# Landing the rotary tables as half runs on 64 partitions and packing them with shuffles and copies

## The chip, the cores and the metric

One core of a Trainium2 chip runs one launch of the kernel. The time is the device time of that launch in microseconds. The profile comes from one execution and gives the span of its work, about 2 us less than the time.

## The reference

A rotary embedding on the first half of each head, with tables of 512 x 32 floats of which only the first 16 columns are used:

```python
# x: (16, 512, 16, 64) float32; cos, sin: (512, 32) float32
x1, x2 = x[..., :32], x[..., 32:]
first  = x1[..., :16] * cos[..., :16] - x1[..., 16:] * sin[..., :16]
second = x1[..., :16] * sin[..., :16] + x1[..., 16:] * cos[..., :16]
return concatenate([first, second, x2], axis=-1)
```

## The kernel before

The 8192 rows of 4 KB are cut into four tiles of 8 MB, 128 partitions by 16 rows (K = 16). A ring of three tiles lies in SBUF. SyncE issues all loads and stores in one queue; VectorE rotates in place; GpSimd issues the two table loads. Partition p of a tile needs the table rows of partition p modulo 32, so the table is landed on 32 partitions and copied to the four groups.

```python
K = 16; T = 4; PB = S // K   # 32
REP = P // PB                # 4
cosf = cos.rearrange("(p k) j -> p (k j)", k=K)       # 32 rows of 2 KB
stage = const_pool.tile([PB, 2, K, HF], fp32)
table = const_pool.tile([P, 2, K, 2, Q], fp32)
# ... (cut)
nc.gpsimd.dma_start(out=stage[:, 0]..., in_=cosf)
nc.gpsimd.dma_start(out=stage[:, 1]..., in_=sinf)
load(0, 0, K0); load(0, K0, K); load(1); load(2, 0, KC)
for r in range(REP):
    nc.vector.tensor_copy(out=table[r * PB : (r + 1) * PB]..., in_=stage[...])
# rotate(): b = x1*s; x1 = x1*c; x1a -= b2; x1b += b1   (four VectorE instructions)
rotate(0, 0, K0); rotate(0, K0, (K0 + K) // 2); rotate(0, (K0 + K) // 2, K)
store(0)
load(2, KC, K)
load(3)                       # takes the place of tile 0, waits for store(0)
for t in range(1, T):
    rotate(t, 0, KC); rotate(t, KC, K); store(t)
```

## Time and profile before

| | before |
|---|---|
| time, median of the first 3 runs | 162.19 us (161.71 to 162.36) |
| span of the profile | 160.1 us |
| DMA queue of the x loads and stores | 97.8% of 16 engines' span |
| VectorE busy | 110.0 us, 69% |
| tables landed, first rotation, first store issued | 9.13, 11.94, 44.14 us |

The lines are shown in the prediction. In them DVE is VectorE, POOL is GpSimd and SPq is SyncE's queue of instructions; q1 is the queue of the x loads and stores and q0 that of the table loads, each with its packets, MB and share of the 16 engines' span.

### The profile page before, as it was taken

What the parts mean: (1) busy time and instruction counts of PE and PEld (TensorE: products, weight loads), DVE (VectorE), ACT (ScalarE), POOL (GpSimd) and SP (SyncE); (2) the same over time, 40 slices, a digit from 0 to 9 for tenths busy, and PEclk for the clock granted to TensorE, in tenths of its full rate; (3) what the DMA queues carried; (4) which work ended last, traced back from release to release, by engine and by line L of the source; (5) the groups of instructions that cost most, each with busy time, mean ns of one, the idle gap of its engine ahead of it and who ended that gap; (6) DMA issues with size and microseconds to landing.
All of it is one profiled execution on the core that took longest, in us unless ns stands there. A gap on an engine that the chain in (4) does not pass through costs nothing.

```text
span 160.1 us, 109 instructions
## 1 busy us (share of the span) xinstructions
DVE 110.0 (69%) x40; POOL 1.3 (1%) x6
## 2 busy tenths in 40 slices
DVE  0069709999999999999999994799999900000000
POOL 3000000000000000000000000000000000000000
DMA  6999999699699799899996996996996996996991
GB/s 197 385 504 454 393 459 524 262 524 491 295 401 581 328 524 409 377 393 418 483 540 295 491 524 262 524 524 262 524 524 262 524 524 262 524 491 295 524 459 66
DMA packets 1504, 67.24 MB, mean 420 GB/s; under 512 B 192, under 2 KB 192, under 8 KB 224
## 3 DMA queue, kind: packets, MB, share of 16 engines
q1 hardware_dynamic: 1440, 67.11, 97.8%
q0 software_dynamic: 64, 0.13, 0.2%
HBM read 33.69 MB, written 33.55 MB: 420 GB/s over the span
## 4 chain that ended last, share of the span: by engine, by line
DMA 50%; DVE 28%; DVEq 1%; issue 0%; SPq 0%
DMA ring<-in_x_dram 32%; DMA out_dram<-ring 18%; DVE b_t L83 10%; DVE ring L84 10%; DVE ring L85 5%; DVE ring L88 3%; DVEq L127 1%; SPq L53 0%; DVEq L83 0%
## 5 line engine op out<-in xcount | busy, mean ns | idle before, releaser
L83 DVE TENSOR_TENSOR b_t<-ring,table 128x4096 f32<-128x4096 f32 (+2 forms) x9 | 35.6, 3959 | 8.2 <-DMA ring<-in_x_dram 8.0
L84 DVE TENSOR_TENSOR ring<-ring,table 128x4096 f32<-128x4096 f32 (+2 forms) x9 | 35.6, 3950 | 0.3
L85 DVE TENSOR_TENSOR ring<-ring,b_t 128x2048 f32<-128x2048 f32 (+2 forms) x9 | 18.4, 2049 | 0.3
L88 DVE TENSOR_TENSOR ring<-ring,b_t 128x2048 f32<-128x2048 f32 (+2 forms) x9 | 18.4, 2042 | 0.0
L67 DVE COPY table<-stage 32x1024 f32<-32x1024 f32 x4 | 2.7, 684 | 9.2 <-DMA stage<-in_sin_dram 9.1
L58 POOL DMA_DIRECT2D stage<-in_cos_dram x1 | 0.6, 631 | 0.8 <-PEq L127 0.8
L59 POOL DMA_DIRECT2D stage<-in_sin_dram x1 | 0.5, 498 | 0.0
L116 POOL MEMSET const-bfloat16-1.0<- 128x1 bf16 x1 | 0.1, 102 | 0.0
L116 POOL MEMSET const-float32-0.0<- 128x1 f32 x1 | 0.1, 99 | 0.2 <-issue 0.2
L116 POOL MEMSET const-float32-1.0<- 128x1 f32 x1 | 0.1, 99 | 0.0
L116 POOL MEMSET const-uint8-127<- 128x1 uint8 x1 | 0.1, 99 | 0.0
## 6 DMA issues: line engine op xcount, KB each, us to landing
ring<-in_x_dram SPq DMA_DIRECT2D x2, 4096.0 KB, 43.9
ring<-in_x_dram SPq DMA_DIRECT2D x1, 6144.0 KB, 22.4
ring<-in_x_dram SPq DMA_DIRECT2D x1, 2048.0 KB, 8.5
stage<-in_cos_dram POOLq DMA_DIRECT2D x1, 64.0 KB, 6.0
stage<-in_sin_dram POOLq DMA_DIRECT2D x1, 64.0 KB, 7.2
out_dram<-ring SPq DMA_DIRECT2D x4, 36.4
ring<-in_x_dram SPq DMA_DIRECT2D x2, 35.0
```

The costliest lines, as they stand in the source:

```text
L58: nc.gpsimd.dma_start(out=stage[:, 0].rearrange("p k j -> p (k j)"), in_=cosf)
L59: nc.gpsimd.dma_start(out=stage[:, 1].rearrange("p k j -> p (k j)"), in_=sinf)
L67: nc.vector.tensor_copy(out=table[r * PB : (r + 1) * PB].rearrange("p t k c j -> p (t k) c j"), in_=stage.rearrange("p t k j -> p (t k) j" ...
L83: nc.vector.tensor_mul(out=b_t, in0=x1, in1=s)
L84: nc.vector.tensor_mul(out=x1, in0=x1, in1=c)
L85: nc.vector.tensor_sub(out=x1[:, :, :, 0:Q], in0=x1[:, :, :, 0:Q], in1=b_t[:, :, :, Q:HF])
L88: nc.vector.tensor_add(out=x1[:, :, :, Q:HF], in0=x1[:, :, :, Q:HF], in1=b_t[:, :, :, 0:Q])
L116: nc = _bacc.Bacc("TRN2", target_bir_lowering=False, num_devices=1)
L127: with _tile.TileContext(nc) as tc:
```

## The change

Its intent is to land each table in 64 rows of 1 KB on 64 partitions in place of 32 rows of 2 KB on 32. Row u of the 64 is half h = u mod 2 of the run of partition u / 2, so the halves have to be brought side by side again. Two shuffles gather the even rows and the odd rows within each group of 32 partitions; two copies bring the upper group's result to partitions 0 to 31 and then overwrite 0 to 15 with the lower group's.

```diff
-    cosf = cos.rearrange("(p k) j -> p (k j)", k=K)
-    sinf = sin.rearrange("(p k) j -> p (k j)", k=K)
+    cosf = cos.rearrange("(u k) j -> u (k j)", k=K // 2)
+    sinf = sin.rearrange("(u k) j -> u (k j)", k=K // 2)
...
-    stage = const_pool.tile([PB, 2, K, HF], fp32)
+    stage = const_pool.tile([2 * PB, 2, K // 2, HF], fp32)
+    spun = const_pool.tile([2 * PB, 2, 2, K // 2, Q], fp32)
+    packed = const_pool.tile([PB, 2, 2, K // 2, Q], fp32)
...
+    for h in range(2):
+        nc.vector.stream_shuffle(
+            out=spun[:, h].rearrange("p t k j -> p (t k) j"),
+            in_=stage.rearrange("p t k j -> p (t k) j")[:, :, 0:Q],
+            mask=[2 * (j % (PB // 2)) + h for j in range(PB)],
+        )
+    for q in (1, 0):
+        n = PB // 2 * (q + 1)
+        nc.vector.tensor_copy(
+            out=packed[0:n], in_=spun[q * PB : q * PB + n].rearrange("p h t k j -> p t h k j")
+        )
...
-            in_=stage.rearrange("p t k j -> p (t k) j")[:, :, 0:Q]
+            in_=packed.rearrange("p t h k j -> p (t h k) j")
```

## The prediction

> **What bounds the kernel now.** I began with the page: its busy shares, its queue lines and its chain.
>
> ```profile
> span 160.1 us, 109 instructions
> DVE 110.0 (69%) x40; POOL 1.3 (1%) x6
> ...
> q1 hardware_dynamic: 1440, 67.11, 97.8%
> q0 software_dynamic: 64, 0.13, 0.2%
> HBM read 33.69 MB, written 33.55 MB: 420 GB/s over the span
> ...
> DMA 50%; DVE 28%; DVEq 1%; issue 0%; SPq 0%
> ```
>
> VectorE is busy for 69% of the span, but the queue that SyncE feeds (all x loads and all stores) has the 16 DMA engines busy for 97.8% of it. So the data transfers are the bound. The chain shows DVE at 28%, which looks as if VectorE time counted. It is misleading here: the chain follows semaphores (a load, the rotation, the store that waits for it), and a store's wait for the rotation costs nothing if the DMA engines still have older work queued. Whether they do is answered by the busy time in stretches (columns: stretch, its length, DVE, POOL, clock, DMA share, GB/s).
>
> ```profile
> 9.20:24.00 14.80, 9.95 (x9) 0.00 (x0) 1.00 1.02 443
> 24.00:44.00 20.00, 19.83 (x8) 0.00 (x0) 1.00 0.97 419
> 44.00:72.00 28.00, 27.76 (x10) 0.00 (x0) 1.00 1.00 431
> 72.00:101.00 29.00, 25.72 (x8) 0.00 (x0) 1.00 1.05 452
> ```
>
> The DMA share is 1.0 within the rounding of stretches from the ninth microsecond on, whatever VectorE does. The packet records of the trace say the same more sharply: from the first packet, 2.0 us into the span, to the last, 156.9 us later, no instant has the queue empty, and the engines hold 16 packets in flight nearly throughout. A 64 KB packet takes 2.42 us; 67.1 MB are 64 such packets on each of 16 engines, which is 155 us of the 160. The end is set by bytes.
>
> The third view is the timeline of the start, which is where the change acts.
>
> ```profile
> 1.25 0.63 POOL L58 DMA_DIRECT2D stage<-in_cos_dram  x1 [0.81 <-PEq L127]
> 1.88 0.50 POOL L59 DMA_DIRECT2D stage<-in_sin_dram  x1
> 9.13 2.77 DVE L67 COPY table<-stage 32x1024 f32<-32x1024 f32 x4 [9.13 <-DMA stage<-in_sin_dram]
> ...
> 17.74 1.21 DVE L88 TENSOR_TENSOR ring<-ring,b_t 128x1024 f32<-128x1024 f32 x1
> 23.66 3.37 DVE L83 TENSOR_TENSOR b_t<-ring,table 128x3072 f32<-128x3072 f32 x1 [4.71 <-DMA ring<-in_x_dram]
> ...
> 42.37 1.75 DVE L88 TENSOR_TENSOR ring<-ring,b_t 128x1536 f32<-128x1536 f32 x1
> 44.14 0.35 SPq L56 DMA_DIRECT2D out_dram<-ring  x1
> ```
>
> Two margins follow. **First margin, 4.71 us:** VectorE gets the tables at 9.13, copies them, rotates the first quarter of tile 0 until 18.95, then sits idle until the rest of tile 0 lands at 23.6. Work added before 18.95 eats this idle time first. **Second margin, some 6.5 us:** the first store is issued at 44.14, but the loads issued before it are not through then. Loads of 20 MB (two tiles of 8 MB and half a third) stand before it, and their last packets end about 50.3 us after the first, at 52.4 us; the store's first packets start at 52.0. From issue to first packet the first load took 1.3 us (0.74 to 2.0), so the store could be issued until about 50.7 without an empty queue: 50.7 less 44.14 is 6.5 us. Later stores have more: the last is issued at 128.1, and its first packet starts at about 139.
>
> **What the Trainium skill says.** Four places bear on the change.
>
> "VectorE: DVE Perf Modes", section "The perf-mode tier table": an fp32 tensor copy in SBUF runs two elements a cycle, a stream shuffle one, about 2400 ns for 2048 elements. The trace agrees for the copy: 1024 elements took 684 ns, while a tensor-tensor on 1024 took 1212, so half the slope on the same fixed part. The shuffle is not in this trace.
>
> "Vector Engine (DVE) Microarchitecture Reference", section 3.8: the shuffle's 32 mask bytes are loaded by an instruction of their own, all banks of 32 lanes apply the same mask, and an operation on at most 32 partitions may read one quadrant and write another. This explains the form of the change: the shuffle cannot bring lanes of quadrant 1 to quadrant 0, so two copies follow. The trace agrees as to moves across quadrants: the four table copies of one quadrant into each of four all take 680 to 686 ns.
>
> "DMA: Bandwidth & Descriptors", section "Queues, rings and completion order": each DMA engine goes round its queues packet by packet. The trace agrees: a table's 4 KB packet took 159 ns, yet the tables landed 6.0 and 7.2 us after issue, since each of their packets waited behind a 16 KB or 48 KB packet of x.
>
> "SBUF — State Buffer", section "SBUF: two separate sides": a VectorE operation in a two-port mode locks GpSimd out of writing descriptors. It cannot matter here: GpSimd has ended its two issues at 2.4 us, and the first VectorE instruction, before and after the change, waits for what these bring.
>
> **The change part by part.** *Moved, the table loads.* Each is still 64 KB on 16 engines, 4 KB an engine, now as 64 rows of 1 KB in place of 32 rows of 2 KB. In DMA time both tables are 32 packets of 0.16 us over 16 engines, 0.3 us an engine; I expect that unchanged, and if the shorter rows doubled it, 0.3 us more. The issue on GpSimd may grow from 0.63 and 0.50 us by some tenths for twice the rows. Landing: unchanged if 4 KB remain one packet; I take 0.3 us later.
>
> *Added, two shuffles.* Each handles 2 tables by 8 rows by 16 columns = 256 elements a partition. At one element a cycle: the tensor-tensor rows give (2292 - 1212)/1024 = 1.05 ns an element and some 140 ns fixed, so 256 x 1.05 + 140 = 0.41 us. From the page's 2400 ns at 2048 the fixed part would be 250 ns and the shuffle 0.52 us. I take 0.46, two of them 0.92. Two mask loads have no duration in the trace; I put 0.1 us for each, 0.2 together, as a guess.
>
> *Added, two copies to 32 and 16 partitions.* 512 elements each; partitions work in parallel, so the smaller one costs the same. From 684 ns for 1024 at two elements a cycle (half of 1.05 ns, so 538 + 146): 512 x 0.525 + 146 = 0.41 us, two 0.83. Were the reordered source to fall to one element a cycle, 0.68 each, which is half a microsecond more in all.
>
> *Kept, the four replications.* Still 32x1024, from a contiguous source now: 684 ns each.
>
> *Removed.* Nothing from VectorE, no byte from the DMA.
>
> Sum on VectorE: 0.92 + 0.20 + 0.83 = 1.95 us, and 0.3 us of later landing: 2.25 us. All of it lies between the landing of sin and the first rotation, which would start at 14.2 in place of 11.94 and end at 21.2 in place of 18.95. The idle time before the second rotation falls from 4.71 to about 2.5 us and that rotation still starts at 23.66 by its load. From there on nothing moves: the first store at 44.1, the end by the DMA bytes. Sum on the path that sets the end: 0, or up to 0.3 if short rows cost DMA time.
>
> **The rivals.** *A, the tables land much later.* If the 64 rows made two packets an engine, each table would wait for one more packet of x; a 48 KB packet takes 1.82 us, so up to 3.6 us for both. With 1.95 us of VectorE work that is 5.6 us, 0.9 beyond the first margin: the first store would be issued at 45.0, still before 50.7. Time: 162.2. For it speaks the slow landing before; against it, that the bytes per engine stay the same.
>
> *B, VectorE becomes the bound at the start.* To reach the end of the kernel the addition must exceed 4.71 + 6.5 = 11.2 us, five times my sum; each microsecond beyond would then cost one. Slower by 2% needs 3.2 us more, 14.4 in all. Nothing in the profile hints at that.
>
> *C, the change pays.* Tables on 64 partitions might land sooner, as the change seems to hope. Even landing at zero would only lengthen the 4.71 us of idle time, since the second rotation starts with its x load. Time: 162.2.
>
> *D, a change of DMA rate.* Different SBUF addresses or another die could move the 2.42 us a packet; the table rows themselves are 0.13 of 67.2 MB. Nothing speaks for it; a tenth of a percent is 0.16 us.
>
> **Range and chances.** The centre is the median before, 162.19, plus nothing: 162.2. The three runs spread from 161.71 to 162.36, that is -0.5 to +0.2; I widen this for another occasion and for up to 0.3 us of DMA time: 161.5 to 163.0. Two per cent would be 3.2 us. Faster would need fewer bytes, and there are none: 0.01. Slower needs rival B: 0.015. Within 2%: 0.975.
>
> **What would show it right or wrong.** Right: the four replications start near 11.4 and keep 684 ns; shuffles of 0.4 to 0.55 us and copies near 0.41; the idle time before the second rotation near 2.5 us, its start still at 23.6 to 23.7; the first store at 44.1; q1 at about 97.8% and 420 GB/s; DVE busy near 112 us. Wrong as to a step: copies near 0.68 (no double rate), sin landing more than a microsecond later (rival A), replications unequal to 684. Wrong altogether: a first store after 50.7, a stretch with a DMA share well below 1 after the ninth microsecond, or a packet time other than 2.42 us.

## The result and the profile after

The changed kernel took 162.31 us (median of 6 runs, 161.75 to 162.52), the kernel before 161.89 us in the same rounds (6 runs). The ratio is 1.0016, with a 95% interval of 0.9995 to 1.0037: no difference is resolved. Ratios here are the mean time of one kernel's fast runs over that of the other's of the same rounds, so they are not quite the ratio of the quoted medians.

The page of the changed kernel, the lines that answer to those of before:

```profile
span 160.1 us, 115 instructions
DVE 111.6 (70%) x46; POOL 1.4 (1%) x6
...
q1 hardware_dynamic: 1440, 67.11, 97.6%
q0 software_dynamic: 64, 0.13, 0.2%
...
DMA 50%; DVE 28%; DVEq 1%; issue 0%; SPq 0%
```

Six instructions and 1.6 us of VectorE work have come in. The span, the packets and bytes of both queues and the shares of the chain are as before. Where the new work went is seen in the timeline of the start (start, duration, engine, line, operation, names, shapes, and in brackets the idle time before it).

```profile
1.89 0.52 POOL L61 DMA_DIRECT2D stage<-in_sin_dram  x1
8.98 0.01 DVE L71 LOAD_MASK_SELECT spun<-stage  x1 [8.98 <-DMA stage<-in_sin_dram]
9.01 0.43 DVE L71 STREAM_SHUFFLE spun<-stage 64x256 f32<-64x256 f32 x1
9.36 0.01 DVE L71 LOAD_MASK_SELECT spun<-stage  x1
9.36 0.43 DVE L71 STREAM_SHUFFLE spun<-stage 64x256 f32<-64x256 f32 x1
9.82 0.86 DVE L78 COPY packed<-spun 32x512 f32<-32x512 f32 x2
10.72 2.77 DVE L83 COPY table<-packed 32x1024 f32<-32x1024 f32 x4
13.53 2.30 DVE L99 TENSOR_TENSOR b_t<-ring,table 128x2048 f32<-128x2048 f32 x1
...
23.37 3.37 DVE L99 TENSOR_TENSOR b_t<-ring,table 128x3072 f32<-128x3072 f32 x1 [2.83 <-DMA ring<-in_x_dram]
...
43.85 0.35 SPq L58 DMA_DIRECT2D out_dram<-ring  x1
```

From the landing of sin to the first rotation it now takes 13.53 - 8.98 = 4.55 us; before it was 11.94 - 9.13 = 2.81. The addition is 1.74 us. The first rotation ends 1.59 us later (20.54 against 18.95), and the idle time after it has shrunk from 4.71 to 2.83 us. The second rotation does not start later: its load sets its start, and that landed 0.29 us earlier in this execution. That is scatter and no gain: in runs below that begin with the same table stage, this rotation starts between 23.31 and 23.73. The first store is issued at 43.85 us, no later than before.

### The profile page after: what moved, and what is told of

Its sections match the earlier page's. It is cut to its first block, busy times and chain, and to the rows that moved or that the text cites. A ratio compares the mean times of both kernels' runs of the same rounds, so it can differ in the third digit from the quotient of the medians.

```text
span 160.1 us, 115 instructions
## 1 busy us (share of the span) xinstructions
DVE 111.6 (70%) x46; POOL 1.4 (1%) x6
## 4 chain that ended last, share of the span: by engine, by line
DMA 50%; DVE 28%; DVEq 1%; issue 0%; SPq 0%
DMA ring<-in_x_dram 32%; DMA out_dram<-ring 18%; DVE b_t L99 10%; DVE ring L100 10%; DVE ring L101 5%; DVE ring L104 3%; DVEq L143 1%; SPq L55 0%; DVEq L99 0%
## 5 line engine op out<-in xcount | busy, mean ns | idle before, releaser
L83 DVE COPY table<-packed 32x1024 f32<-32x1024 f32 x4 | 2.7, 683 | 0.1
L78 DVE COPY packed<-spun 32x512 f32<-32x512 f32 (+1 forms) x2 | 0.8, 416 | 0.1
L71 DVE STREAM_SHUFFLE spun<-stage 64x256 f32<-64x256 f32 x2 | 0.8, 430 | 0.0
```

Source lines behind the costliest of these rows:

```text
L71: nc.vector.stream_shuffle(out=spun[:, h].rearrange("p t k j -> p (t k) j"), in_=stage.rearrange("p t k j -> p (t k) j")[:, :, 0:Q], mask= ...
L78: nc.vector.tensor_copy(out=packed[0:n], in_=spun[q * PB : q * PB + n].rearrange("p h t k j -> p t h k j"))
L83: nc.vector.tensor_copy(out=table[r * PB : (r + 1) * PB].rearrange("p t k c j -> p (t k) c j"), in_=packed.rearrange("p t h k j -> p (t h ...
```

## The experiments

My theory was: the bytes through the DMA queue set the end, and what VectorE does before the first store is hidden by two margins in turn, the idle time before the second rotation and the work still queued when the first store is issued. The main rival was that VectorE's chain sets the end (the chain of the profile gives it 28%) and that only the idle time hid the addition. Chips differed between the batches, so each run is compared with the kernel before in its own rounds; those medians were 162.01, 162.06 and 161.84 us.

### Nothing on VectorE at the start: no_table_stage

```diff
-    for r in range(REP):
-        nc.vector.tensor_copy(out=table[...], in_=stage[...])
+    nc.vector.memset(table, 1.0)
```

> The kernel before with the four replications and their wait for the tables taken away; a memset at the start fills the table instead (wrong result on purpose; the table loads stay, unread). My theory: the first rotation starts when the first quarter of tile 0 lands, near 9.2 us, in place of 11.94; the idle time before the second rotation grows from 4.71 to about 7.4 us; time 162.2, ratio 1.00. Rival (the table stage counts, so undoing it pays): 2.8 us less, 159.4, ratio 0.983.

Measured: 162.01 us, ratio 1.0003 (0.9986 to 1.0020). Its timeline:

```profile
9.36 2.30 DVE L77 TENSOR_TENSOR b_t<-ring,table 128x2048 f32<-128x2048 f32 x1 [7.42 <-DMA ring<-in_x_dram]
...
23.68 3.37 DVE L77 TENSOR_TENSOR b_t<-ring,table 128x3072 f32<-128x3072 f32 x1 [7.32 <-DMA ring<-in_x_dram]
```

The whole table stage can vanish and the time stays; the 2.6 us gained turn into idle time before the second rotation. So no other way of landing or packing the tables can pay in this kernel, however good. (The table loads themselves stayed; their packets are 0.3 us of each DMA engine's time.)

### Less of VectorE's work everywhere: less_vector

```diff
-        nc.vector.tensor_sub(out=x1[:, :, :, 0:Q], ...)
-        nc.vector.tensor_add(out=x1[:, :, :, Q:HF], ...)
```

> The changed kernel without the subtraction and the addition of each rotation (wrong result on purpose): VectorE loses 18 instructions and 36.8 of 111.6 us. My theory: the first store is issued some 7 us earlier, the queue was full anyway, the DMA share stays near 0.98, time 162.2, ratio 1.00. Rival (the 28% of VectorE in the chain that ended last are on the path): up to 10 us less, 152, ratio 0.94.

Measured: 162.19 us, ratio 1.0008 (0.9991 to 1.0025). The page:

```profile
DVE 75.2 (47%) x28; POOL 1.4 (1%) x6
...
q1 hardware_dynamic: 1440, 67.11, 97.7%
...
DMA 54%; DVE 19%; SPq 0%; issue 0%
```

VectorE lost 36 us and its share of the chain fell from 28 to 19%, while the time stayed. So the chain's VectorE share was not time that sets the end. The chain follows who released whom, and does not show that the released store then stood in a queue.

### Fewer bytes: less_bytes

```diff
-        store(t)
+        store(t, 0, K if t < T - 1 else KC)
```

> The changed kernel whose last store leaves out the second half of its rows, 4 MB of 64 (wrong result on purpose: the rest of the output is not written). My theory: the end moves by what 8 packets of 32 KB on each engine take, 8 x 1.21 = 9.7 us: 152.5, ratio 0.940. Rival (the last store waits for VectorE, whose last rotation ends at 128 us, so the tail is latency): clearly less than 9.7 us.

Measured: 152.83 us, ratio 0.9431 (0.9417 to 0.9445). That is 9.2 us less (0.0569 of 162.06) where 9.7 was worked out from the packets. Leaving out bytes moves the end nearly one for one, and nothing else tried shortened it.

### More work before the first rotation: after_rep2, after_rep3, after_rep4, after_rep6, before_rep6

Each repeats the four replications, which keeps the result correct and adds 2.8 us of VectorE work a time. after_rep2 was run after the other four, whose results its expectation quotes. The edit of after_rep3, the others alike:

```diff
-    for r in range(REP):
+    for r in [i % REP for i in range(4 * REP)]:
```

> The changed kernel with the replications three times over (8 more copies, 5.5 us more VectorE work). The first store should be issued near 46.6 us, 4 us before the point where the queue runs dry. By the two margins alone: 162.2, ratio 1.00. The run with 8.3 us more had no hole in the queue and was yet 1.5 us longer, with the last 64 KB packets before the two switches of direction near 70 and 98 us stretched from 2.42 to up to 3.75 us; if that sets in as soon as the first margin is gone, this run is about 0.5 to 1.0 us longer than the kernel before, ratio 1.003 to 1.006.

> The changed kernel with its four replications done four times over in place of once: 12 more copies at 0.69 us, 8.3 us more VectorE work ahead of the first rotation, same result. My theory (DMA bytes set the end, VectorE has two margins): 2.83 us of idle time before the second rotation are left, so that rotation starts 5.5 us late, the first store is issued near 49.3 us in place of 43.85, still before about 50.7, the queue never runs dry, time 162.2 (ratio to the kernel before 1.00). Rival (VectorE's chain sets the end, and the change was hidden only by the idle time before the second rotation): 5.5 us longer, about 167.7, ratio 1.034.

> The changed kernel with the replications five times over: 16 more copies, 11.1 us more VectorE work. My theory: first store issued near 52.1 us, about 1.4 us past the point (some 50.7) from which the queue runs dry; this is near the knee, so time 162.2 plus 0.3 to 1.8, ratio 1.002 to 1.011. Rival (VectorE's chain sets the end): 8.2 us longer, 170.4, ratio 1.05.

> The changed kernel with the replications seven times over: 24 more copies, 16.6 us more VectorE work. My theory: first store issued near 57.6 us, 6.9 us past the point where the queue runs dry, so the time is 162.2 + 6.9 = 169.1, ratio 1.043, and the trace shows a hole of nearly 7 us in the DMA work from about 52 us. Rival (VectorE's chain sets the end): 13.8 us longer, 176, ratio 1.085. Third theory (DMA bound whatever VectorE does): 162.2.

> The kernel before with the replications seven times over, 16.6 us more VectorE work: past both margins, so that what the change adds can be seen. My theory: first store near 56.0 us, 5.3 us past the point where the queue runs dry, time 167.5; and the changed kernel with the same addition is longer by what the change adds ahead of the first rotation, 1.6 us (169.1). If the change's cost were hidden by something other than the two margins, the two would take the same time.

Measured, with the hole (the time in which no packet of the x queue is under way) and the number of 64 KB packets of over 2.8 us (of 768) from the packet records:

| kernel | first store issued, us | hole, us | long packets | longest, us | time, us | ratio |
|---|---|---|---|---|---|---|
| changed kernel | 43.85 | none | 0 | 2.69 | 162.31 | 1.0016 |
| after_rep2 | 47.08 | none | 1 | 2.90 | 162.43 | 1.0034 |
| after_rep3 | 49.75 | none | 20 | 3.75 | 163.53 | 1.0093 |
| after_rep4 | 52.31 | 1.43 | 32 | 3.77 | 165.36 | 1.0205 |
| after_rep6 | 58.02 | 7.09 | 32 | 4.13 | 172.32 | 1.0631 |
| before_rep6 | 56.58 | 5.43 | 33 | 4.31 | 170.42 | 1.0514 |

The hole can be seen in the busy time by stretches. First after_rep6 (columns as in the prediction: DVE, POOL, clock, DMA share, GB/s), then before_rep6:

```profile
44.00:52.00 8.00, 7.90 (x5) 0.00 (x0) 1.00 0.91 393
52.00:59.00 7.00, 6.93 (x4) 0.00 (x0) 1.00 0.33 140
59.00:72.00 13.00, 12.90 (x5) 0.00 (x0) 1.00 0.94 408
```

```profile
44.00:52.00 8.00, 7.93 (x4) 0.00 (x0) 1.00 0.91 393
52.00:57.00 5.00, 4.93 (x4) 0.00 (x0) 1.00 0.00 0
57.00:72.00 15.00, 14.90 (x5) 0.00 (x0) 1.00 1.01 437
```

In before_rep6 nothing moves from 52 to 57 us, since the loads are through and the first store has not come. In after_rep6 the table's exact hole is the better figure; the 0.33 of its stretch are packets that start at the very end of it, from 58.86 us, and are counted with their whole time where they start.

Three things follow. **First, the theory of two margins comes nearer than both rivals.** VectorE's chain as the bound would have made after_rep3, rep4 and rep6 5.5, 8.2 and 13.8 us longer; they were 1.5, 3.3 and 10.2 longer by the ratios. A kernel bound by DMA whatever VectorE does would have stayed at 162. The holes were forecast well (1.4, 6.9 and 5.3 us expected for after_rep4, after_rep6 and before_rep6), but the times of the four with a first store after 49 us all came out above what I had expected: 163.53 against 162.2, 165.36 against 162.5 to 164.0, 172.32 against 169.1, 170.42 against 167.5. **Second, the cost of the change can be seen once the margins are used up.** With the same repetitions in both, the changed kernel was 1.8 us longer than the kernel before (mean 172.28 against 170.45; the two profiled executions alone differ by 1.3 us in span), and its added instructions take 1.74 us. **Third, my figure for the second margin was too generous.** The store's first packet follows its issue by 0.84 us when the queue is empty (after_rep4, after_rep6 and before_rep6 alike), and the first engine is free at 51.70 us in the kernel before, so the queue runs dry only when the store comes after 50.9 us. But after_rep3, with its store at 49.75 and no hole, already lost 1.5 us, and the runs with a hole lost about 2 to 3 us beyond it (10.2 against 7.1, 8.3 against 5.4, 3.3 against 1.4). A good part lies in stretched packets: the last 64 KB packet of each engine before the switch from storing to loading near 70 us, and before the one from loading to storing near 98 us. Their excess over 2.42 us, summed and divided by 16 engines, is 0.2 and 0.9 us in after_rep3. That is a mean, and the end is that of the slowest engine: the last packets of the 16 engines end 1.7 us apart there, 0.6 apart in the changed kernel.

### What stretches the packets: rep3_light, busy_tail, late_store2

Besides the late first store itself (theory 3), two other things differ near 98 us in after_rep3: VectorE is busy there (theory 1), and the store of tile 2 is not yet queued (theory 2). late_store2 was meant to hold that store back.

```diff
 rep3_light = after_rep3 and, in rotate():
+        if t > 0:
+            return
         nc.vector.tensor_sub(...)
```

```diff
 busy_tail
         store(t)
+        if t == 2:
+            nc.vector.tensor_mul(out=b_full, in0=ring[:, 2, 0:KC, :, 0:HF], in1=Sn...)
```

```diff
 late_store2
         rotate(t, 0, KC)
+        if t == 3:
+            nc.vector.tensor_scalar_mul(out=cell, in0=cell, scalar1=1.0)   # one column of tile 2
+            store(2)
         rotate(t, KC, K)
-        store(t)
+        if t != 2:
+            store(t)
```

> The changed kernel with the replications four times over, and without the subtraction and addition from tile 1 on (wrong result on purpose): the first store is as late as in the run with four replications (49.7 us), but VectorE is done with tile 2 near 85 us, so its store is queued and VectorE is idle when the last load ends near 100 us. If the stretched packets near 98 us come of VectorE being busy then (theory 1) or of the next store not being queued yet (theory 2), they are gone: 0.9 of the 1.5 us go, ratio about 1.003. If they come of the late first store itself (theory 3), they stay: ratio about 1.009.

> The changed kernel with one more 128x4096 multiplication into the scratch buffer after the store of tile 2 is issued (97.6 us), so that VectorE is busy over the end of the last load, and the store is queued in time (correct result). Theory 1 (busy VectorE stretches the last packets): up to 0.9 us longer, ratio 1.005. Theories 2 and 3: 162.2, ratio 1.00.

> The changed kernel whose store of tile 2 is held back until the first half of tile 3 is rotated (near 115 us in place of 97.6), by a multiplication of one column of tile 2 by one (correct result); the queue still holds the store of tile 1 until 120 us. Theory 2 (the next store must be queued when the direction switches): 0.9 us longer, ratio 1.005, with stretched packets near 98 us. Theories 1 and 3: 162.2, ratio 1.00.

Measured: rep3_light 164.51 us, ratio 1.0161 (1.0125 to 1.0197); busy_tail 162.11, ratio 1.0016 (1.0001 to 1.0031); late_store2 162.12, ratio 1.0019 (1.0004 to 1.0034).

The edit of late_store2 did not do what it was meant to. Two stretches of its timeline:

```profile
57.55 0.15 DVE L118 TENSOR_SCALAR ring<-ring 128x1 f32<-128x1 f32 x1
...
98.00 0.34 SPq L58 DMA_DIRECT2D out_dram<-ring  x1
```

The multiplication ran at 57.55 us, before tile 2 was rotated, and the store of tile 2 was issued at 98.00 and not near 115, hardly later than the changed kernel's 97.64. (Why it ran so early is not shown; its column is one that no rotation writes.) So this run does not test theory 2. after_rep2 does:

```profile
98.55 2.28 DVE L104 TENSOR_TENSOR ring<-ring,b_t 128x2048 f32<-128x2048 f32 x1
100.86 0.34 SPq L58 DMA_DIRECT2D out_dram<-ring  x1
```

There VectorE was busy over the switch near 98 us and the store of tile 2 came only at 100.86, and yet one packet alone in the whole run took over 2.8 us (2.90, at 108 us).

The timeline of rep3_light shows that its store of tile 2 was queued early and VectorE idle over the switch:

```profile
91.34 0.34 SPq L58 DMA_DIRECT2D out_dram<-ring  x1
103.28 4.43 DVE L99 TENSOR_TENSOR b_t<-ring,table 128x4096 f32<-128x4096 f32 x1 [11.96 <-DMA ring<-in_x_dram]
```

Yet its stretched packets near 98 us were there, with 1.1 us of excess, and the time was longer still than after_rep3's. In busy_tail no packet took over 2.7 us, and its ratio is the changed kernel's own 1.0016. So theories 1 and 2 fall: rep3_light has the stretched packets without either of their causes, and after_rep2 has both causes with hardly a stretched packet. The loss goes with a first store that is issued late against the loads queued before it, setting in between 47.1 us (after_rep2, whose ratio of 1.0034, 1.0019 to 1.0049, cannot be told from the changed kernel's) and 49.75 us. SyncE issues the load of the rest of tile 2 0.39 us behind that store in each of these kernels, so no run tells the late store from this late load. Why the engines stretch a packet some 20 and 50 us after that stays open; no run here shows its mechanism.

### The shuffle's rate: wide_shuffle

```diff
+    nc.vector.stream_shuffle(
+        out=table[0:64]...,                       # 1024 elements, overwritten later
+        in_=ring[0:64, 0, 0]..., mask=list(range(32)))
```

> The changed kernel with one more shuffle, of 1024 elements on 64 partitions, from the first rows of tile 0 into the table ahead of its replication (correct result). It measures the slope of a shuffle: if it goes at the rate of a tensor-tensor (1.05 ns an element, 140 to 160 ns fixed) it takes 1.22 to 1.24 us beside 0.43 for 256 elements; if the fixed part is larger[...], 1.3 or more. Time unchanged, 162.2, as 1.3 us fit in the 2.83 us of idle time.

One look (a single run, state unknown): 162.19 us, correct. The timeline:

```profile
9.32 0.43 DVE L76 STREAM_SHUFFLE spun<-stage 64x256 f32<-64x256 f32 x1
...
12.10 1.28 DVE L70 STREAM_SHUFFLE table<-ring 64x1024 f32<-64x1024 f32 x1
```

The wide shuffle took 1.28 us: (1.28 - 0.43)/768 = 1.11 ns an element and 0.15 us fixed, an estimate from two shuffles of one execution that read differently laid out tiles. That lies between what I had put down for the two theories: the fixed part is the small one, and the slope is a little above a tensor-tensor's 1.05 ns.

## Why the prediction was right

The time was forecast at 162.2 us and measured at 162.31; by the ratio the change does nothing that 6 runs resolve. (A cost of some 0.3 us stays possible: busy_tail and late_store2, with the changed kernel's table stage, have intervals that just exclude 1.) The agreement of the time does not test the sum of the added work, since a sum of double the size would have been hidden as well; the timeline tests it. The steps:

- **The bound.** Right, and shown twice: less_bytes moved the end by nearly what the missing packets take, and less_vector did not move it at all.
- **The sum of the added work.** Forecast 1.95 us, measured 1.74. The copies were right (0.416 and 0.415 us against 0.41); with 683 ns for 1024 elements that is 0.52 ns an element, so the half slope, which one size could only suggest, is now shown. The shuffles took 0.43 us each against 0.46, and the second starts 0.35 us after the first, so that they overlap a little. The mask loads, a guess of 0.1 us each, are 5 to 14 ns. The replications stayed at 683 ns and began at 10.72 us in place of 11.4.
- **The landing.** Forecast 0.3 us later; sin landed 7.0 us after its issue in place of 7.2. As the forecast said, the packets stayed the same in number and size (64, 0.13 MB), and rival A's extra packet did not come about. The issue on GpSimd grew by only 0.02 us each. The reason that the prediction gives for the slow landing covers only a part of it: in the packet records of the kernel before, the first table packet starts at 5.34 us, 4.1 us after the issue of cos, and from there on table packets stand behind 16 KB packets of x of 0.6 to 0.9 us, none behind one of 48 KB. What fills the 4.1 us is not shown.
- **The first margin.** Forecast to shrink to about 2.5 us, measured 2.83; the difference is the smaller sum and the landing, less 0.3 us by which the x load came early.
- **The second margin.** It was not needed for the result: the first store came at 43.85 us. The prediction's packet times lie some 0.25 us late on the profile's axis (the first x packet starts at 1.75 us and not at 2.0, the first store packet at 51.7 and not at 52.0); this cancels in the 50.7 us. Tested by itself it was too large as I had put it. "Each microsecond beyond would then cost one" left out the stretched packets: after_rep3 lost 1.5 us before the queue ran dry, and before_rep6, with 17.2 us more than the kernel before ahead of the first rotation, lost 8.3 us where the two margins' 11.2 us would have left 6.0.
- **Rival C.** no_table_stage, which has no table stage at all, shows that no better landing could have paid.

## What to carry to other kernels

Before costing an added instruction, find out what stands in the queue behind which its result will wait: if the DMA engines hold work until well after the store is issued, VectorE work is free up to that point, and neither a 69% busy engine nor its share of the chain of releases says otherwise. Take the margin as smaller than the moment at which the queue would run dry, as coming close to it already cost about 1% here. And when the queue is full from its first packet to its last, look to the bytes first: moving fewer of them was the only edit here that made the kernel faster. A higher rate of the packets was not tried.

## What the Trainium skill lacked or had wrong

- "Vector Engine (DVE) Microarchitecture Reference", section 3.8, names the instruction that loads the shuffle's mask but gives it no time: it took 5 to 14 ns here, and a shuffle could start 0.35 us after one of 0.43 us in spite of the mask load between them.
- "VectorE: DVE Perf Modes", section "The perf-mode tier table", gives a shuffle's time at one size. The runs add 0.43 us at 256 and 1.28 us at 1024 elements a partition, both on 64 partitions. Carried on at 1.11 ns an element this gives an estimated 2.41 us at 2048, in agreement with the page's 2400 ns (given under bf16); the page's number is therefore not to be read as a large fixed part.
- "DMA: Bandwidth & Descriptors", section "Where 436 GB/s comes from", says that the HBM side, at about 358 GB/s, binds transfers between HBM and SBUF. On this one core it did not: 420 GB/s over the whole span, loads and stores, and 2.418 us for a 64 KB packet on each of 16 engines, which is 434 GB/s, near the page's 435 for the fabric. It is this sentence that is too wide, not the page: just before it, the page has 425 GB/s for one core alone and keeps 358 for two cores that stream at once.
- No page read for this case has the loss by a transfer that is queued late behind others of the opposite direction: 20 to 33 packets of up to 4.3 us in place of 2.42 at later switches of direction, and in after_rep3 1.5 us of time without any hole in the queue.
